# Retention in chunks of 64 on quarters of the matrix array, with query products ahead of the head transposes

## The chip, the cores and the metric

The kernel runs on one core of a Trainium2 chip. A core has a matrix engine (TensorE, PE in the profile) with an array of 128 x 128 cells, a vector engine (VectorE, DVE), a scalar engine (ScalarE, ACT), GpSimd (POOL), and a queue engine for transfers (SyncE, SP). Working memory (SBUF) has 128 partitions; TensorE writes its results to banks of PSUM, from which VectorE and ScalarE read. The metric is the device time of one execution in microseconds.

## What is computed

The reference is a trunk of two layers over 1024 frames of 1024 channels. Layer 0 holds a state-space branch and a retention branch, layer 1 a convolution module. The change touches retention alone:

```python
CHUNK = 64; RET_HEADS = 8; RET_DK = 64; RET_DV = 128
scores = einsum('bnihd,bnjhd->bnhij', qc, kc) * intra       # within a chunk of 64
intra_out = einsum('bnhij,bnjhe->bnihe', scores, vc)
kv = einsum('bnjhd,jh,bnjhe->bnhde', kc, k_dec, vc)         # one state per chunk
# state_step: s -> chunk_decay * s + kv_n, and chunk n sees the state before it
cross = einsum('bnihd,ih,bnhde->bnihe', qc, q_dec, s_prev)
out = intra_out + cross                                      # then normalised per head
```

Queries and keys are rotated by position first, and the normalised output is multiplied by a SiLU gate. All of it is f32.

## The kernel before, in words

The eight heads are worked on in four pairs. A pair's keys lie in a tile of 128 partitions (two heads of 64 channels) by 1024 frames, and so do its queries. The value tiles `vt` have frames on partitions.

`retention` (line 936) runs over the pairs. For each it takes the finished rotated keys and queries of `ret_proj`, emits six pieces of `weight_low`, starts `ret_proj` of the next pair up to its key products, and then emits `ret_heads`. `weight_low` (line 224) is work for layer 1: it loads half a weight block, casts it on ScalarE, subtracts on GpSimd and stores the low part, in two buffers for each tile. The next pair's query products come only when the loop comes round.

`ret_proj` (line 974) makes 48 products of 512 columns for the keys and 48 for the queries (`mm_k`, `mm_q`, lines 276 to 278: each block is multiplied as high and low parts, three products a block). VectorE scales them (line 987), four transfers swap halves of the rotation (line 996), GpSimd multiplies by the tables and VectorE adds (line 1003).

`ret_heads` (line 1079) works on blocks of 128 frames, that is two chunks:

- eight transposes of the keys (`ktp`, line 1088), each group of four multiplied by the key decay on VectorE (line 1090);
- the products `kv` (line 1107): a block's 128 frames are contracted, the output has 64 rows a head, so the two heads take the two column halves of the array;
- the recurrence of the states `S` on VectorE (lines 1115 and 1117), seven links, one per block;
- the scores `sp` (line 1124): 64 channels are contracted, so the two heads take the two row halves; VectorE masks them into `sc` (line 1130). The mask is zero where a frame of the first chunk would see the second;
- the outputs `ro`: state products on row halves (line 1154), then value products on the whole array (line 1159), each half of the sequence in two PSUM banks, one a head;
- per head and half: mean and variance (lines 1168 and 1169), the root on ScalarE (line 552), normalising (line 1174), transposes back (`rt`, line 1182), the multiplication by the gates `grl` (line 1185), and a store (line 1188).

Every engine works through its instructions in order. The order is fixed when the kernel is built: a planner takes instructions by their place in the program, the earlier first, and fills an engine's idle time, as it estimates it, with later ones that are ready. `issue_after(x)` puts an instruction behind x where both are on the same engine; `chained` fixes the order of a list of products. Five PSUM banks (`ps_aux`) serve all the tiles of `ret_heads`, three (`ps_mm`) the projections. After retention come the gated linear unit of the state-space branch (`mm_glu`), the output projection and layer 1.

Of the kernel before, what the change touches and what calls it, by code (L numbers as in the profile page):

```python
# [19 lines left out]
P = 128  # L20
D = 1024
T = 1024
# [35 lines left out]
class Trunk:  # L58
# [877 lines left out]
    def retention(self, st):  # L936
# [7 lines left out]
        self.mask = r0.tile([P, NH, P], F32, name="retmask")  # L944
        nc.sync.dma_start(self.mask[:], A["ret_mask"])
        self.g128 = r0.tile([P, 4], F32, name="g128")
        nc.sync.dma_start(self.g128[:], A["ret_g128"])
        self.kdec = r0.tile([P, NH, 64], F32, name="kdec")
# [3 lines left out]
        ahead = None  # L952
        for pair in range(4):
            cur = list(ahead or self.ret_proj(pair))[-1]
            if pair == 0:
                with ExitStack() as vst:
                    V = self.ret_values(self.pool("vp", 1, stack=vst))
                self.rp = self.pool("ret", 1, stack=st)
                ry = self.pool("retl", 1, stack=early, side="right")
            with ExitStack() as held:  # L960
# [12 lines left out]

# [46 lines left out]
    def ret_values(self, vp):  # L1020
# [56 lines left out]
        return lambda p, b, hh: vt[p // 2][b // 4][:, b % 4, (2 * (p % 2) + hh) * P:(2 * (p % 2) + hh + 1) * P]  # L1077

    def ret_heads(self, pair, K, Q, qadds, V, turned):
# [4 lines left out]
        for hf in range(2):  # L1084
            ps = self.bank(f"ktp{hf}_{pair}")
            for b in range(4):
                t0 = (4 * hf + b) * P
                nc.tensor.transpose(ps[:, b * P:(b + 1) * P], K[:, t0:t0 + P], self.ident[:])
            kd = self.kdec[:, 2 * pair:2 * pair + 2, :].rearrange("p h d -> p (h d)")
            self.last_kt = v.tensor_tensor(kt[:, 4 * hf:4 * hf + 4, :], ps[:].rearrange("p (b d) -> p b d", b=4),  # L1090
                                           kd.unsqueeze(1).broadcast_to([P, 4, P]), op=ALU.mult)
# [6 lines left out]
        S = rp.tile([P, 8, P], F32, name=f"S_{pair}", tag="S", bufs=1)  # L1098
        for hf in range(2):
            ps = self.bank(f"kv{hf}_{pair}")  # L1100
            for b4 in range(4):
                b = 4 * hf + b4
                if b == 7:
                    continue
                for hh in range(2):
                    r = slice(64 * hh, 64 * hh + 64)
                    nc.tensor.matmul(ps[r, b4 * P:(b4 + 1) * P], kt[:, b, r], V(pair, b, hh),
                                     start=True, stop=True)
            for b4 in range(4):
                b = 4 * hf + b4  # L1110
                if b == 7:
                    continue
                kv = ps[:, b4 * P:(b4 + 1) * P]
                if b == 0:
                    v.tensor_copy(S[:, 1, :], kv)
                else:
                    v.scalar_tensor_tensor(S[:, b + 1, :], S[:, b, :], self.g128[:, pair:pair + 1], kv,
                                           op0=ALU.mult, op1=ALU.add)

        self.masked = [None, None]  # L1120
        sc = [rp.tile([P, 8, P], F32, name=f"sc{hh}_{pair}", tag=f"sc{hh}", bufs=1) for hh in range(2)]
        for hf in range(2):
            sps = [self.bank(f"sp{hf}{hh}_{pair}") for hh in range(2)]
            self.chained(nc.tensor.matmul(sps[hh][:, b4 * P:(b4 + 1) * P],
                                          K[64 * hh:64 * hh + 64, (4 * hf + b4) * P:(4 * hf + b4 + 1) * P],
                                          Q[64 * hh:64 * hh + 64, (4 * hf + b4) * P:(4 * hf + b4 + 1) * P],
                                          start=True, stop=True)
                         for b4 in range(4) for hh in range(2))
            for hh in range(2):
                self.masked[hf] = v.tensor_tensor(  # L1130
                    sc[hh][:, 4 * hf:4 * hf + 4, :], sps[hh][:].rearrange("p (b i) -> p b i", b=4),
                    self.mask[:, 2 * pair + hh, :].unsqueeze(1).broadcast_to([P, 4, P]), op=ALU.mult)

# [4 lines left out]
        for hh in range(2):  # L1138
            h = 2 * pair + hh
            gt = rp.tile([P, T], F32, name=f"grl_{h}", tag="grl", bufs=3)  # L1140
# [4 lines left out]
        for hf in range(2):  # L1145
            pss = [self.bank(f"ro{hf}_{2 * pair + hh}") for hh in range(2)]

            def products():
                for b4 in range(4):
                    b = 4 * hf + b4  # L1150
                    for hh in range(2):
                        r = slice(64 * hh, 64 * hh + 64)
                        if b:
                            yield nc.tensor.matmul(pss[hh][:, b4 * P:(b4 + 1) * P], Q[r, b * P:(b + 1) * P],
                                                   S[r, b, :], start=b4 == (hf == 0), stop=False)
                for hh in range(2):
# [615 lines left out]
```

## Time and profile before

| | us |
|---|---|
| median of three runs (1176.0 to 1176.86) | 1176.35 |
| the profiled execution, first to last instruction | 1173.9 |
| TensorE busy in it | 1161.3 |
| VectorE busy | 910.5 |
| GpSimd busy | 713.5 |
| ScalarE busy | 545.1 |

Only the span of the profiled execution is given; the runs' time lies 2.45 us above it. In the rows of the profile a line number (L1159) points into the kernel, `ro<-v,sc` names the tile written and the tiles read, `64*128` the part of the array used (rows times columns), and a bracket the idle time of the engine before the instruction, with what ended it. PEld is TensorE's loading of the stationary operand, which runs beside its products. In a table of stretches each row is a window in us, the busy time of the engines with their instructions, the clock that TensorE was granted (1.00 is full), the share of the transfer engines, and GB/s. One transfer engine's queue is written SPq.

### The profile page before, as it was taken

Reading aid. Unit: us, or ns where it says so; the run is one execution under the profiler, and the core shown is the slowest. Engines: PE = TensorE matmul, PEld = TensorE weight load, DVE = VectorE, ACT = ScalarE, POOL = GpSimd, SP = SyncE. Lnnn points to the kernel's source line nnn. Section 1 sums busy time; section 2 is a strip of 40 time slices with the busy share of each in tenths; the row PEclk is TensorE's granted clock in tenths of the full one; section 3 lists DMA queues with packets and bytes.
Section 4 is the critical chain, followed back from the end, with each engine's and each line's share of the span. In section 5 each row is a group of like instructions: output and inputs, shape, how many; then the busy total and the mean of one; then the engine's idle time right before and its main releaser. Section 6 shows DMA issues by size and latency. Waiting matters only on the chain.

```text
span 1173.9 us, 17492 instructions
## 1 busy us (share of the span) xinstructions
PE 1161.3 (99%) x6150; PEld 965.5 (82%) x6150; DVE 910.5 (78%) x1507; ACT 545.1 (46%) x821; POOL 713.5 (61%) x507
## 2 busy tenths in 40 slices
PE   9999999999999999999999999999999999999997
PEld 7888888888888888887788888888888888888887
DVE  7875789999717475689777888479999999999643
ACT  7212343332226642123645544367756678544662
POOL 2049999888843245664444034348894689977742
PEclk9999999999999999999999999999999999999999
DMA  9353378778789765765988468965448553357863
GB/s 344 109 178 109 134 270 312 272 269 282 273 307 325 268 228 192 251 190 180 362 313 304 160 220 268 309 232 188 161 158 306 216 182 132 134 176 243 281 247 138
DMA packets 131192, 270.66 MB, mean 231 GB/s; under 512 B 12832, under 2 KB 41760, under 8 KB 130976
## 3 DMA queue, kind: packets, MB, share of 16 engines
q1 hardware_dynamic: 129952, 265.35, 66.5%
q10 hardware_dynamic: 1152, 4.19, 0.9%
q8 instruction: 48, 0.79, 0.3%
q14 instruction: 40, 0.33, 0.1%
HBM read 193.54 MB, written 71.76 MB: 226 GB/s over the span
## 4 chain that ended last, share of the span: by engine, by line
PE 91%; DMA 4%; DVE 2%; SPq 1%; ACT 1%; POOL 1%; issue 1%; DVEq 0%; POOLq 0%; ACTq 0%
PE mm_g L277 8%; PE mm_g L278 8%; PE mm_g L276 7%; PE mm_w L278 4%; PE mm_w L277 4%; PE mm_w L276 4%; PE mm_a L278 2%; PE mm_b L277 2%; PE mm_a L276 2%; PE mm_b L278 2%; PE mm_a L277 2%; PE mm_b L276 2%; PE mm_u L278 2%; PE mm_oc L278 2%; PE mm_u L277 2%; PE mm_oc L277 2%
## 5 line engine op out<-in xcount | busy, mean ns | idle before, releaser
L1461 DVE SCALAR_TENSOR_TENSOR cv<-u,convw,cv 128x512 f32<-128x512 f32 x358 | 244.7, 750 | 5.0 <-ACT cv L1447 3.5
L1441 POOL TENSOR_TENSOR tp<-tp,tp 128x512 f32<-128x512 f32 x104 | 138.9, 1338 | 28.7 <-ACT tp L1440 23.4
L278 PE MATMUL mm_g<-xh,wl_g 128*128 128x512 f32 x256 | 100.8, 394 | 0.0
L277 PE MATMUL mm_g<-xl,wh_g 128*128 128x512 f32 x256 | 100.7, 394 | 0.0
L276 PE MATMUL mm_g<-xh,wh_g 128*128 128x512 f32 x256 | 100.5, 393 | 0.0
L1440 ACT ACTIVATE tp<-u,convw 128x512 f32<-128x512 f32 x104 | 69.6, 713 | 9.6 <-POOL tp L1441 9.4
L277 PEld LDWEIGHTS mm_g<-xl,wh_g 128*128 128x128 f32 x256 | 48.1, 188 | 11.2 <-issue 1.6
L278 PEld LDWEIGHTS mm_g<-xh,wl_g 128*128 128x128 f32 x256 | 48.0, 188 | 10.5
L276 PEld LDWEIGHTS mm_g<-xh,wh_g 128*128 128x128 f32 x256 | 48.1, 188 | 9.6
L278 PE MATMUL mm_oc<-zh,wl_woc 128*128 128x512 f32 (+1 forms) x152 | 54.5, 360 | 0.2 <-DMA wl_woc<-lo_woc 0.2
L276 PE MATMUL mm_oc<-zh,wh_woc 128*128 128x512 f32 (+1 forms) x152 | 54.3, 362 | 0.0
L277 PE MATMUL mm_oc<-zl,wh_woc 128*128 128x512 f32 (+1 forms) x152 | 54.0, 357 | 0.0
L276 PE MATMUL mm_glu<-yh,wh_glu 128*128 128x512 f32 x128 | 50.0, 392 | 1.3 <-ACT sg L1250 1.3
L277 PE MATMUL mm_u<-xl,wh_u 128*128 128x512 f32 x128 | 50.1, 391 | 1.0 <-DVE xl L390 0.9
L276 PE MATMUL mm_g<-h1h,wh_cg 128*128 128x512 f32 x128 | 50.3, 393 | 0.0
L276 PE MATMUL mm_a<-h1h,wh_ca 128*128 128x512 f32 x128 | 50.3, 393 | 0.0
L278 PE MATMUL mm_b<-h1h,wl_cb 128*128 128x512 f32 x128 | 50.3, 393 | 0.0
L232 ACT CAST lh<-lf 128x512 fp32r<-128x512 f32 x32 | 19.5, 618 | 65.9 <-DMA lf<-w_c 59.3
L278 PE MATMUL mm_a<-h1h,wl_ca 128*128 128x512 f32 x128 | 50.0, 391 | 0.0
L277 PE MATMUL mm_glu<-yl,wh_glu 128*128 128x512 f32 x128 | 50.0, 392 | 0.0
L278 PE MATMUL mm_g<-h1h,wl_cg 128*128 128x512 f32 x128 | 49.9, 390 | 0.0
L277 PE MATMUL mm_g<-h1l,wh_cg 128*128 128x512 f32 x128 | 49.9, 390 | 0.0
(811 smaller groups left out, 3637.3 us busy)
## 6 DMA issues: line engine op xcount, KB each, us to landing
wf_g<-w_ab SPq DMA_DIRECT2D x16, 512.0 KB, 5.4
a<-w_out SPq DMA_DIRECT2D x32, 256.0 KB, 4.4
ws<-a SPq DMA_DIRECT2D x32, 256.0 KB, 4.8
lf<-w_c SPq DMA_DIRECT2D x32, 256.0 KB, 5.3
wf_p<-ws SPq DMA_DIRECT2D x16, 512.0 KB, 4.1
wf_cb<-w_c SPq DMA_DIRECT2D x16, 512.0 KB, 4.9
wf_ca<-w_c SPq DMA_DIRECT2D x16, 512.0 KB, 4.7
wl_cb<-lo_cb SPq DMA_DIRECT2D x16, 512.0 KB, 3.4
```

What stands on the lines that cost most here:

```text
L232: self.nc.scalar.copy(hi[:], f[:])
L276: nc.tensor.matmul(ps, wh[:, kb, :], xh, start=start, stop=False)
L277: nc.tensor.matmul(ps, wh[:, kb, :], xl, start=False, stop=False)
L278: self.last_mm = nc.tensor.matmul(ps, wl[:, kb, :], xh, start=False, stop=stop)
L1440: nc.scalar.mul(sk[:], u[:, k:k + HALF], cw[:, nb, k:k + 1])
L1441: gp.tensor_tensor(s0[:], s0[:], sk[:], op=ALU.add)
L1461: v.scalar_tensor_tensor(dst[:], *tap, accs_[i][:], op0=ALU.mult, op1=ALU.add)
```

## The change

Retention goes from blocks of 128 frames to chunks of 64, as in the reference:

- The scores of chunk c are made by 64 x 64 pieces of keys and queries; head 0 takes the upper left quarter of the array and head 1 the lower right. Both heads' scores lie in one tile `sc`, head 0 on the lower partitions and head 1 on the upper, and in one bank for eight chunks. The mask is a table of 64 columns a pair, without zeros.
- `kv`, the state products and the value products are 64 x 64 in the stationary operand and 128 columns in the moving one, so each takes a quarter; four successive ones take four different quarters. `kv` uses four banks a pair.
- `S` has 15 states, and the recurrence 15 links with the decay of 64 frames.
- A value product needs a chunk's values on the partitions of its head's scores. For odd chunks of head 0 and even chunks of head 1 they lie on the other half, so `crossed` copies them into a tile `vx` (one buffer) with four transfers a pair, after the values for pair 0 and after `ret_heads` of the pair before for the others.
- Statistics of both halves are emitted before the first three normalisations; then the next pair's query products with all that follows them (`fill`); then two transposes groups, the fourth normalisation, and the last two groups.
- The six low parts a pair go into two groups of three, one where all six stood and one behind the key transposes (`last_kt`), with three buffers.
- The gates have two buffers instead of three, the statistics' small tiles four instead of two; the tables for mask and key decay shrink.

```diff
-            held.enter_context(self.tc.issue_after((self.last_rs if pair else self.last_sum).ins))
-            for k in range(LOWS * pair // 3, LOWS * (pair + 1) // 3) if pair < 3 else ():
-                self.weight_low(ry, k, (("la", "lb"), ("la", "lb")), 2, nc.gpsimd)
+            def lows(n, behind):
+                with self.tc.issue_after(behind.ins):
+                    for k in range(n * LOWS // 6, (n + 1) * LOWS // 6) if pair < 3 else ():
+                        self.weight_low(ry, k, (("la", "lb"), ("la", "lb")), 3, nc.gpsimd)
             def turned():
+                lows(2 * pair + 1, self.last_kt)
...
+            lows(2 * pair, self.last_rs if pair else self.last_sum)
...
-            self.ret_heads(pair, *cur, V, turned)
+            cur = self.ret_heads(pair, *cur, V, turned, lambda: list(ahead)[-1] if ahead else None)
+            if pair < 3:
+                self.crossed(pair + 1)
...
+    def crossed(self, pair):
+        d, i = pair // 2, pair % 2
+        self.vx = self.r0.tile([P, 8, P], F32, name=f"vx{pair}", tag="vx", bufs=1)
+        for h in range(2):
+            for hh in range(2):
+                to, of = slice(64 * hh, 64 * hh + 64), slice(64 - 64 * hh, 128 - 64 * hh)
+                self.nc.sync.dma_start(self.vx[to, 4 * h:4 * h + 4, :],
+                                       self.vt[d][h][of, :, (2 * i + hh) * P:(2 * i + hh + 1) * P])
...
+            kvs = [self.bank(f"kv{hf}{par}_{pair}") for par in range(2)]
+            self.chained(nc.tensor.matmul(kvs[c % 2][half(hh), col(c)], kt[half(c % 2), c // 2, half(hh)],
+                                          V(pair, c, hh)[half(c % 2)], start=True, stop=True)
+                         for c in cs for hh in range(2))
...
+            sps = self.bank(f"sp{hf}_{pair}")[:].rearrange("p (c i) -> p c i", c=8)
+            self.chained(nc.tensor.matmul(sps[half(hh), c % 8, :], K[half(hh), tok(c)], Q[half(hh), tok(c)],
                                           start=True, stop=True)
+                         for c in range(8 * hf, 8 * hf + 8) for hh in range(2))
...
+                            yield nc.tensor.matmul(out(c, hh), Q[half(hh), tok(c)], S[half(hh), c - 1, :],
+                                                   start=c in (2, 1, 8, 9), stop=False)
+                for c in cs:
+                    for hh in range(2):
+                        yield nc.tensor.matmul(out(c, hh), sc[half(hh), c, :], V(pair, c, hh, True)[half(hh)],
+                                               start=False, stop=c % 8 > 5)
...
+        on00, on01, on10 = (normed(*a) for a in todo[:3])
+        nxt = fill()
+        last_ro = turn(0, 1, on01, last_ro)
+        last_ro = turn(0, 0, on00, last_ro)
+        on11 = normed(*todo[3])
+        last_ro = turn(1, 0, on10, last_ro)
+        turn(1, 1, on11, last_ro)
```

More of the change, by code (lines that the diff above doesn't have):

```diff
@@ L951, in retention @@
         nc.sync.dma_start(self.reps[:], A["ret_eps"])
-        ahead = None
+        cur = list(self.ret_proj(0))[-1]
         for pair in range(4):
-            cur = list(ahead or self.ret_proj(pair))[-1]
             if pair == 0:
@@ L1076, in ret_values, with value, ret_heads @@
                     self.y_pass(vp, cb)
-        return lambda p, b, hh: vt[p // 2][b // 4][:, b % 4, (2 * (p % 2) + hh) * P:(2 * (p % 2) + hh + 1) * P]
-    def ret_heads(self, pair, K, Q, qadds, V, turned):
+        def value(p, c, hh, own=False):
+            d, h, b, i = p // 2, c // 8, c // 2 % 4, p % 2
+            if own and c % 2 != hh:
+                return self.vx[:, c // 2, :]
+            return vt[d][h][:, b, (2 * i + hh) * P:(2 * i + hh + 1) * P]
+        return value
+    def crossed(self, pair):
[6 more added lines that the diff above has]
+                                       self.vt[d][h][of, :, (2 * i + hh) * P:(2 * i + hh + 1) * P])
+    def ret_heads(self, pair, K, Q, qadds, V, turned, fill):
         nc, rp = self.nc, self.rp
@@ L1096, in ret_heads @@
         turned()
-        S = rp.tile([P, 8, P], F32, name=f"S_{pair}", tag="S", bufs=1)
+        S = rp.tile([P, 15, P], F32, name=f"S_{pair}", tag="S", bufs=1)
+        half = lambda i: slice(64 * i, 64 * i + 64)
         for hf in range(2):
[L1100 to L1115, printed above, removed]
+            kvs = [self.bank(f"kv{hf}{par}_{pair}") for par in range(2)]
+            cs = [c for c in range(8 * hf, 8 * hf + 8) if c < 15]
+            col = lambda c: slice(c // 2 % 4 * P, (c // 2 % 4 + 1) * P)
+            self.chained(nc.tensor.matmul(kvs[c % 2][half(hh), col(c)], kt[half(c % 2), c // 2, half(hh)],
+                                          V(pair, c, hh)[half(c % 2)], start=True, stop=True)
+                         for c in cs for hh in range(2))
+            for c in cs:
+                kv = kvs[c % 2][:, col(c)]
+                if c == 0:
+                    v.tensor_copy(S[:, 0, :], kv)
@@ L1116, in ret_heads @@
                 else:
-                    v.scalar_tensor_tensor(S[:, b + 1, :], S[:, b, :], self.g128[:, pair:pair + 1], kv,
+                    v.scalar_tensor_tensor(S[:, c, :], S[:, c - 1, :], self.g64[:, pair:pair + 1], kv,
                                            op0=ALU.mult, op1=ALU.add)
         self.masked = [None, None]
-        sc = [rp.tile([P, 8, P], F32, name=f"sc{hh}_{pair}", tag=f"sc{hh}", bufs=1) for hh in range(2)]
+        sc = rp.tile([P, 16, 64], F32, name=f"sc_{pair}", tag="sc", bufs=1)
@@ L1122, in ret_heads @@
         for hf in range(2):
[L1123 to L1126, printed above, removed]
+            sps = self.bank(f"sp{hf}_{pair}")[:].rearrange("p (c i) -> p c i", c=8)
+            tok = lambda c: slice(c * 64, (c + 1) * 64)
@@ L1139, in ret_heads @@
             h = 2 * pair + hh
[L1140 removed]
+            gt = rp.tile([P, T], F32, name=f"grl_{h}", tag="grl", bufs=2)
             with self.tc.issue_after(self.masked[0].ins):
@@ L1148, in products @@
             def products():
-                for b4 in range(4):
-                    b = 4 * hf + b4
+                cs = range(8 * hf, 8 * hf + 8)
+                out = lambda c, hh: pss[hh][half(c % 2), c // 2 % 4 * P:(c // 2 % 4 + 1) * P]
+                for c in cs:
                     for hh in range(2):
[L1152 to L1156, printed above, removed]
-                    for b4 in range(4):
-                        b = 4 * hf + b4
-                        yield nc.tensor.matmul(pss[hh][:, b4 * P:(b4 + 1) * P], sc[hh][:, b, :],
-                                               V(pair, b, hh), start=False, stop=b4 == 3)
+                        if c:
+                            yield nc.tensor.matmul(out(c, hh), Q[half(hh), tok(c)], S[half(hh), c - 1, :],
+                                                   start=c in (2, 1, 8, 9), stop=False)
+                for c in cs:
+                    for hh in range(2):
+                        yield nc.tensor.matmul(out(c, hh), sc[half(hh), c, :], V(pair, c, hh, True)[half(hh)],
+                                               start=False, stop=c % 8 > 5)
             last_ro = self.chained(products())
```

70 lines of the change are left out of this document (35 added, 35 removed).

## The prediction

> **What bounds the kernel now.** I read the page first, then the busy time by stretches, then TensorE's instructions in order of time.
>
> ```profile
> span 1173.9 us, 17492 instructions
> PE 1161.3 (99%) x6150; PEld 965.5 (82%) x6150; DVE 910.5 (78%) x1507; ACT 545.1 (46%) x821; POOL 713.5 (61%) x507
> ...
> PE 91%; DMA 4%; DVE 2%; SPq 1%; ACT 1%; POOL 1%; issue 1%; DVEq 0%; POOLq 0%; ACTq 0%
> ```
>
> TensorE is busy for 99% of the span, and 91% of the chain that ended last is its work. In the stretches of 25 us it runs 112 products of 512 columns back to back, or 0.223 us each; only retention (448 to 592 us) leaves something over:
>
> ```profile
> 475.00:500.00 25.00, 25.00 (x192) 21.23 (x191) 16.20 (x45) 3.37 (x6) 17.57 (x13) 1.00 0.81 253
> 525.00:550.00 25.00, 23.96 (x154) 20.15 (x153) 24.03 (x70) 7.59 (x16) 11.29 (x8) 1.00 0.63 184
> 550.00:575.00 25.00, 24.05 (x190) 20.13 (x188) 20.46 (x60) 9.21 (x13) 9.55 (x7) 1.00 0.85 312
> 600.00:625.00 25.00, 25.00 (x112) 20.73 (x111) 16.74 (x25) 11.54 (x18) 12.59 (x6) 1.00 0.92 323
> ```
>
> The waits there, from TensorE's order of time, sum to 3.0 us, and VectorE ends two of the three:
>
> ```profile
> 544.83 1.06 PE L1182 MATMUL rt<-ident,on 128*128 128x128 f32 x8 [1.04 <-DVE on L1174]
> 553.95 1.75 PE L1107 MATMUL kv<-v,kt 128*64 128x128 f32 x28 [0.67 <-DVE kt L1090]
> 576.05 0.50 PE L276 MATMUL mm_glu<-yh,wh_glu 128*128 128x512 f32 x1 [1.33 <-ACT sg L1250]
> ```
>
> So the end moves by what TensorE is spared, less any wait that appears. TensorE is just as full after retention, so what is won there should reach the end undiminished.
>
> **What the small products cost now.** Pair 0 in order of time, with one line that stands for the filler from the next pair's projection:
>
> ```profile
> 447.49 1.75 PE L1107 MATMUL kv<-v,kt 128*64 128x128 f32 x28
> 449.17 1.38 PE L1124 MATMUL sp<-qrot,krot 64*128 64x128 f32 x18
> 450.48 0.51 PE L276 MATMUL mm_q<-xh,wh_q 128*128 128x512 f32 x1
> ...
> 452.77 1.04 PE L1124 MATMUL sp<-qrot,krot 64*128 64x128 f32 x13
> ...
> 454.53 2.05 PE L1159 MATMUL ro<-v,sc 128*128 128x128 f32 x16
> 456.51 1.16 PE L1154 MATMUL ro<-S,qrot 64*128 64x128 f32 x16
> 457.60 2.05 PE L1159 MATMUL ro<-v,sc 128*128 128x128 f32 x16
> 459.41 0.48 PE L276 MATMUL mm_q<-xh,wh_q 128*128 128x512 f32 x1
> ```
>
> Every f32 product stands as two instructions (line 1107 makes 14 a pair, the row shows 28). I take times from start to start. Sixteen full-array instructions last 454.53 to 456.51, 1.98 us; sixteen on halves of the array, two at a time, last 1.09 us. If a step of the array (one set of parallel instructions) lasts t and a change of the array's partition s, then 16t + s = 1.98 and 8t + s = 1.09: t = 0.111, s = 0.20 us. The block kv agrees roughly: 14t + s = 1.75 against 1.68.
>
> A pair takes 447.49 to 450.48 and 452.77 to 459.41, or 9.63 us. In steps that is kv 14, scores 16, state products 14, values 32: 76t = 8.44 us, with about seven changes of partition.
>
> **Four at a time?** No row of before has 64x64 quarters. The nearest are four column strips of S5:
>
> ```profile
> 108.80 0.45 PE L882 MATMUL kp<-Mr,s_s_cbr 128*32 128x128 f32 x8
> 109.04 0.42 PE L883 MATMUL kp<-Mi,s_s_cbi 128*32 128x128 f32 x8
> 109.39 0.50 PE L277 MATMUL mm_g<-xl,wh_g 128*128 128x512 f32 x1
> 108.79 0.18 PEld L882 LDWEIGHTS kp<-Mr,s_s_cbr 128*32 128x32 f32 x8 [0.17 <-issue]
> ```
>
> Eight start within 0.24 us, and all sixteen with the change of partition behind them last 0.59 us (4t + s = 0.64). Four run at once, 0.03 us each, so issue is no floor. Row pairs (sp, ro) and column pairs (kv) run together too. I therefore take 0.111 us for four quarters; the other bound is two at a time.
>
> *A rule that speaks against it.* The Trainium skill (TensorE: Matmul & The Clock Gate, Part 3: Packing small matmuls, The mechanism) says that a weight load overlaps running products only where the row group differs; two quarters of one row group would then be taken in turn, which is the last rival below. Here the trace differs: the eight loads of kp share all rows and were under way within 0.18 us.
>
> **The change, part by part.**
>
> *Products.* kv has 15 chunks x 2 heads = 30 products, 60 instructions, 15 steps. State products: 30, 15 steps. Values: 32 products of half the contraction and half the tokens, 16 steps instead of 32. Scores: 32 products with 64 columns, but only on the two diagonal quarters: 32 short steps. How long is a short step?
>
> ```profile
> L1159 PEld LDWEIGHTS ro<-v,sc x128: 185/192/193, 454.5 to 570.2; 128*128 128x128 f32 x128
> L1107 PEld LDWEIGHTS kv<-v,kt x112: 132/137/138, 447.5 to 555.3; 128*64 128x64 f32 x112
> ...
> 34.95 1.73 PE ss L547 x16
> ```
>
> The last line, from the chain, is a product with 64 moving columns and 128 columns of weights: 0.108 us each, so halving the moving side alone wins nothing. But the load of 64 columns is 0.055 us shorter than that of 128 (137 against 192 ns), half a step, and here both sides are halved. Bounds 0.055 and 0.111 us; I take 0.055, that is 16t. Sum after: 15 + 15 + 16 + 16 = 62t = 6.88 us. All four kinds now have one partition; with one filler in between there are four changes, 0.80 us. 7.68 against 9.63: 1.95 us a pair, **8 us** in four pairs (bounds: 12.6 us lost if quarters run two at a time, 0.9 us won if score steps stay long; both are rivals below).
>
> *VectorE.* The recurrence grows from 7 links to 15, the masks halve from four instructions to two:
>
> ```profile
> L1117 DVE SCALAR_TENSOR_TENSOR S<-S,g,kv x24: 336/347/348, 449.0 to 565.4; 128x128 f32<-128x128 f32 x24
> L1130 DVE TENSOR_TENSOR sc<-sp,retmask x16: 680/684/692, 450.8 to 566.3; 128x512 f32<-128x512 f32 x16
> ```
>
> 8 x 0.347 - 2 x 0.684 = +1.4 us a pair. From the first kv half (8t = 0.9 us) the chain ends after 0.9 + 15 x 0.347 + two masks 1.4 = 7.5 us; TensorE has kv, scores and the first half of the outputs in that time (15t + 16t + 15t = 5.1 us), so it needs about 2.4 us of projection between them, as much as the 2.29 us it puts there now (450.48 to 452.77). In pairs 0 and 1 that cover is there, and VectorE is a third idle (16.20 of 25). In 525 to 550 us it has 24.03 of 25: there I let one pair's 1.4 us come through as a wait, **+1.5 us**. The key decay and the normalisations keep their counts, and the smaller tables are loaded once, long before use.
>
> *Queries in front of the transposes.* All 48 query products of the next pair are the same work. Of them some 38 (8.5 us) are left when the outputs are done, where now 6.66 us pass before the first transposes:
>
> ```profile
> 466.07 1.06 PE L1182 MATMUL rt<-ident,on 128*128 128x128 f32 x8 [0.27 <-DVE mv L1169]
> L1168 DVE BATCH_NORM_STATS2 st<-ro 128x6 f32<-128x128 f32 x64 | 14.3, 279 | 1.4 <-PE ro L1159 1.4
> L1174 DVE TENSOR_SCALAR on<-ro,mv,rs 128x128 f32<-128x128 f32 x64 | 21.7, 403 | 0.3
> ```
>
> Three normalisations must now precede the first transpose (3/4 x 21.7/4 = 4.1 us, behind 3.6 us of statistics): 7.7 us, which 8.5 us cover. Without that cover it costs the difference to the gate products that stand in, up to 1.3 us as for sg above. What is late next is the product with the gates and its store. Cost: nothing. The three waits of before may go (-3.0) or stay; I keep them.
>
> *Copies and low parts.*
>
> ```profile
> L996 SPq DMA_DIRECT2D kswp<-kraw x16: 507/583/616, 354.1 to 522.2; - x16
> kswp<-kraw SPq DMA_DIRECT2D x16, 128.0 KB, 3.9
> ...
> DMA to landing us min/median/max: 2.3/3.3/7.7
> L232 ACT CAST lh<-lf 128x512 fp32r<-128x512 f32 x32 | 19.5, 618 | 65.9 <-DMA lf<-w_c 59.3
> ```
>
> Each pair adds four copies within SBUF of 128 KB, as large as those of kswp: 4 x 0.58 = 2.3 us of SP's queue, landing 3 to 8 us later. They wait for the previous pair's last value product (the tile has one buffer); behind them in SP's queue stand the swapped copies of the next keys and the low parts' loads. They are read a whole pair's projection later (96 x 0.223 = 21 us), which hides them; without it TensorE would wait up to 7.7 us. The low parts are the same 18 loads, casts (0.618 us) and subtractions, spread wider and with a third buffer; nothing on TensorE reads them here, their loads only fill DMA time. The gates' loads with two buffers wait for both stores, 20 us ahead of use. All taken as nothing.
>
> **Sum.** In the profiled execution's terms 1173.9 - 8.0 + 1.5 = 1167.4 us. The median of the runs, 1176.35, lies 2.45 above that span, so the forecast is **1169.9 us**, 6.5 less.
>
> **The rivals.**
>
> 1. *The short score step does not halve.* Then scores cost 32t, 1.8 us more a pair: 1169.9 + 7.1 = 1177.0. The product of line 547 speaks for it, the shorter weight load against it. The Trainium skill (TensorEngine Tiling (Array Packing), Gotcha 1: PSUM Pressure) gives a mechanism with the same price: different row tiles cannot use one PSUM bank at once, and the two heads' scores now share a bank. No row tells: each row pair of before writes two banks.
>
> 2. *The recurrence is uncovered (the other side).* Place: between kv and the second half of the state products, in every pair. The eight links more are 8 x 0.347 = 2.8 us; where the order fixed beforehand holds no projection for them TensorE waits that long. Price 4 x 2.8 = 11.2: 1176.35 - 8 + 11.2 = 1179.5. It decides from 2.0 us a pair on, where it eats the gain. For it speaks pair 3, where the seven links took 8.4 us because other VectorE work stood between; against it, that projections are free to be put there.
>
> ```profile
> 557.41 0.29 DVE L1115 COPY S<-kv 128x128 f32<-128x128 f32 x1
> ...
> 565.03 0.73 DVE L1117 SCALAR_TENSOR_TENSOR S<-S,g,kv 128x128 f32<-128x128 f32 x2
> ```
>
> 3. *Quarters run two at a time.* 30 + 30 + 32 + 16 = 108t = 12.0 + 0.8 against 9.63, +3.2 us a pair: 1176.35 + 12.6 = 1189. Break-even lies at 79 steps. The rows of kp speak against it.
>
> 4. *The waits of before go as well.* 1176.35 - 8.0 - 3.0 = 1165.3; for it speak the earlier queries, against it VectorE's 24.03 of 25.
>
> **How the numbers follow.** Forecast 0.52 (its own range 1166 to 1174), rivals in order 0.14, 0.14, 0.10, 0.10. The measurement tells 0.2%, 2.35 us. Faster: forecast and rival 4, 0.62. Same: rival 1 and the part of rival 2 with half of the chain covered, 0.14 + 0.04 = 0.18. Slower: rest of rival 2 and rival 3, 0.20. The range 1164 to 1180 leaves out rival 3 and the thin ends.
>
> **What would show it.** kv, ro and sp rows of form 64*64, 60 to 64 a pair; kv and ro blocks of 0.03 us an instruction (0.055 is rival 3); score blocks of 0.9 us for 32 instructions (1.8 is rival 1); 60 recurrence links, and no TensorE wait on S of over 1 us (rival 2 would show about 2.8 us each); VectorE's sum up by some 5.6 us. Wrong it would be above all if TensorE's idle time in retention grows by more than the 8 us.

## The result, and the profile after

The changed kernel takes 1192.22 us (median of four runs, 1188.89 to 1192.88), the kernel before 1176.61 us beside it. The ratio is 1.0118, with an interval of 1.0097 to 1.0138: slower by 1.2%, or about 14 us, where 6.5 us less was forecast. The medians lie 15.6 us apart, the two profiled executions 17.2 us. The page's head, the busy sums and the chain's shares:

```profile
span 1191.1 us, 18558 instructions
...
PE 1161.4 (98%) x6662; PEld 965.3 (81%) x6662; DVE 927.1 (78%) x1531; ACT 539.4 (45%) x817; POOL 711.4 (60%) x507
...
PE 81%; DMA 9%; DVE 4%; SPq 2%; POOL 2%; issue 2%; ACT 1%; DVEq 0%; ACTq 0%; POOLq 0%
```

TensorE's share of the chain fell from 91% to 81%, and transfers and VectorE took its place. Where, the stretches show (busy time of the engines in their fixed order, then the granted clock):

```profile
475.00:500.00 25.00, 25.00 (x331) 21.16 (x330) 19.35 (x54) 1.61 (x3) 9.30 (x6) 1.00 0.73 207
500.00:525.00 25.00, 23.06 (x186) 19.11 (x185) 18.34 (x43) 7.88 (x14) 23.51 (x16) 0.93 0.68 207
525.00:550.00 25.00, 20.25 (x218) 16.74 (x218) 23.41 (x71) 7.81 (x15) 9.30 (x6) 0.89 0.72 205
550.00:575.00 25.00, 19.84 (x242) 16.89 (x244) 17.96 (x40) 3.28 (x5) 5.99 (x5) 0.84 0.69 240
575.00:600.00 25.00, 18.32 (x141) 15.17 (x134) 19.05 (x65) 10.87 (x17) 8.55 (x5) 0.86 0.86 300
600.00:625.00 25.00, 25.00 (x112) 20.69 (x111) 23.03 (x22) 10.76 (x17) 14.22 (x8) 1.00 0.93 336
```

From 500 to 600 us TensorE stands still for 100 - 81.47 = 18.5 us, against 3.0 before. The clock, 1.00 in all of these rows before, is 0.84 to 0.93. Little is lost elsewhere.

The array's part did what was forecast. Pair 0 in TensorE's order of time (start and duration first, then engine, line and operation):

```profile
448.13 1.85 PE L1125 MATMUL kv<-v,kt 64*64 64x128 f32 x58
...
449.93 1.09 PE L1141 MATMUL sp<-qrot,krot 64*64 64x64 f32 x30
450.95 0.50 PE L276 MATMUL mm_q<-xh,wh_q 128*128 128x512 f32 x1
...
453.67 0.97 PE L1141 MATMUL sp<-qrot,krot 64*64 64x64 f32 x26
...
457.93 0.38 PE L1170 MATMUL ro<-v,sc 64*64 64x128 f32 x2
458.24 0.50 PE L278 MATMUL mm_q<-xh,wl_q 128*128 128x512 f32 x1
```

2.82 and 4.57 us make 7.39 us for the pair (7.68 forecast, 9.63 before). What was lost is in the rows with a bracket:

```profile
509.28 0.63 PE L1195 MATMUL rt<-ident,on 128*128 128x128 f32 x4 [1.94 <-DVE rs L553]
...
545.76 1.94 PE L1195 MATMUL rt<-ident,on 128*128 128x128 f32 x8 [4.32 <-DVE mv L1180]
550.06 0.63 PE L277 MATMUL mm_glu<-yl,wh_glu 128*128 128x512 f32 x1
550.49 0.63 PE L278 MATMUL mm_glu<-yh,wl_glu 128*128 128x512 f32 x1
...
571.67 2.13 PE L1166 MATMUL ro<-S,qrot 64*64 64x128 f32 x27 [5.17 <-DVE S L1133]
584.26 1.97 PE L1195 MATMUL rt<-ident,on 128*128 128x128 f32 x8 [6.56 <-DVE on L1189]
```

Two things cost here: the waits, and what follows them. The eight transposes after the 4.32 us take 1.94 us where such a group took 1.06 us before, and the products of 512 columns behind them start 0.43 us apart instead of 0.223: half speed. The books for TensorE from its first `kv` to its first `mm_w` (start 447.5 and 643.3 before, 448.1 and 659.2 after): 15.3 us longer = 15.1 of waits (the brackets sum to 18.4 against 3.3) - 6.7 of small products (31.8 against 38.5, from start to start) + 6.9 in the rows of the transposes and the projections, which are the same work as before at a lower clock.

**Why pair 3 waits.** VectorE names `S` and the normalisations, but is itself held up. Its queue in pair 3, then SP's:

```profile
566.32 0.69 DVE L1273 SCALAR_TENSOR_TENSOR sg<-sg,yg 128x512 f32<-128x512 f32 x1 [2.93 <-POOL yg L1268]
566.93 1.11 DVE L1133 SCALAR_TENSOR_TENSOR S<-S,g,kv 128x128 f32<-128x128 f32 x3
569.35 0.69 DVE L1216 TENSOR_TENSOR yl<-yf,yh 128x512 fp32r<-128x512 f32 x1 [1.31 <-ACT yh L1214]
...
576.69 0.69 DVE L233 TENSOR_TENSOR lh<-lf,lh 128x512 fp32r<-128x512 f32 x1 [1.54 <-ACT lh L232]
```

```profile
553.55 0.32 SPq L1209 DMA_DIRECT2D yr_d<-grl  x1
558.20 0.33 SPq L1154 DMA_DIRECT2D grl<-gr_d  x1
558.62 0.38 SPq L1209 DMA_DIRECT2D yr_d<-grl  x1
...
563.68 0.32 SPq L1154 DMA_DIRECT2D grl<-gr_d  x1
564.10 0.85 SPq L1245 DMA_DIRECT2D yf<-yn_d  x2
```

Read the second block first. With two gate buffers pair 3's first load of gates (558.20) needs pair 2's first store to have landed, 4.6 us after its issue. Pair 2's second store was ready at 556.3 but stands behind that load and goes at 558.62; the second load then needs that store, until 563.68. So two store latencies come one after the other, and the next stage's rows `yf` behind them go at 564.10 (558.25 before). ScalarE's cast of the rows waits for them, GpSimd's `yg` waits for `yn` from the same queue, and the work on VectorE that needs both (`sg`, `yl`) stands between the links of `S`. Pair 2's wait has another cause and is followed below.

**Why pair 1 waits.** The same happens two pairs earlier, with pair 0's stores:

```profile
486.92 0.38 SPq L1209 DMA_DIRECT2D yr_d<-grl  x1
487.40 0.51 SPq L1001 DMA_DIRECT2D kswp<-kraw  x1
494.05 0.32 SPq L1154 DMA_DIRECT2D grl<-gr_d  x1
494.42 1.79 SPq L1001 DMA_DIRECT2D kswp<-kraw  x3
```

Pair 1's second load of gates needs pair 0's second store and goes 7.1 us behind it; three of the four swapped copies of the next keys stand behind that load. GpSimd takes the copies up at 500.55, VectorE waits 2.13 us for the product and starts to add it at 504.39, and the normalisation behind it is late for the transposes at 509.28 (the wait of 1.94 us).

### The profile page after: what moved, and what is told of

It reads as the page before. It is cut to its first block, busy times and chain, and to the rows that moved or that the text cites. A ratio compares the mean times of both kernels' runs of the same rounds, so it can differ in the third digit from the quotient of the medians.

```text
span 1191.1 us, 18558 instructions
## 1 busy us (share of the span) xinstructions
PE 1161.4 (98%) x6662; PEld 965.3 (81%) x6662; DVE 927.1 (78%) x1531; ACT 539.4 (45%) x817; POOL 711.4 (60%) x507
## 4 chain that ended last, share of the span: by engine, by line
PE 81%; DMA 9%; DVE 4%; SPq 2%; POOL 2%; issue 2%; ACT 1%; DVEq 0%; ACTq 0%; POOLq 0%
PE mm_g L277 7%; PE mm_g L278 7%; PE mm_g L276 7%; PE mm_w L278 4%; PE mm_w L277 4%; PE mm_w L276 4%; DMA lf<-w_c 3%; PE mm_a L278 2%; PE mm_b L278 2%; PE mm_b L277 2%; PE mm_a L277 2%; PE mm_a L276 2%; PE mm_b L276 2%; PE mm_u L278 2%; PE mm_oc L278 2%; PE mm_u L277 2%
## 5 line engine op out<-in xcount | busy, mean ns | idle before, releaser
L1268 POOL TENSOR_TENSOR yg<-yg,yn 128x512 f32<-128x512 f32 x16 | 23.2, 1455 | 56.6 <-DMA yn<-yn_d 17.6
L278 PE MATMUL mm_glu<-yh,wl_glu 128*128 128x512 f32 x128 | 51.4, 401 | 0.0
L276 PE MATMUL mm_u<-xh,wh_u 128*128 128x512 f32 x128 | 49.2, 396 | 1.3 <-ACT xh L389 1.3
```

Of the source, the lines that this page charges most:

```text
L276: nc.tensor.matmul(ps, wh[:, kb, :], xh, start=start, stop=False)
L278: self.last_mm = nc.tensor.matmul(ps, wl[:, kb, :], xh, start=False, stop=stop)
L1268: gp.tensor_tensor(yg[:], yg[:], yn[:], op=ALU.mult)
```

## The experiments

All ratios are to the kernel before, run beside each. Three kernels leave work out, so that their output is not the reference's: e_nocopy (the copies), e_short and e_short_links (8 of the 16 value products a pair).

| kernel | ratio, interval | us |
|---|---|---|
| e_rest: the change without the quarters | 1.0003, 0.999 to 1.0015 | 1178.67 |
| e_before_fill: before + queries in front | 0.9989, 0.9978 to 1.0001 | 1176.40 |
| e_before_gates2: before + two gate buffers | 0.9992, 0.9982 to 1.0002 | 1176.16 |
| e_quarters: quarters and copies alone | 1.0111, 1.0093 to 1.0128 | 1190.45 |
| e_low6: quarters + queries in front | 1.0082, 1.0067 to 1.0097 | 1186.78 |
| e_gates3_early: that + low parts in threes, third buffer | 1.0012, 1.0000 to 1.0024 | 1179.59 |
| e_early: that + two gate buffers | 1.0003, 0.9993 to 1.0012 | 1178.03 |
| changed kernel: that + late normalisations | 1.0118, 1.0097 to 1.0138 | 1192.22 |
| e_gates3: changed, three gate buffers | 1.0078, 1.0058 to 1.0099 | 1187.39 |
| e_hold: changed, pair 3's transposes later | 1.0151, 1.0125 to 1.0178 | 1195.60 |
| e_nocopy: changed, without the copies | 1.0111, 1.0092 to 1.0131 | 1190.86 |
| e_after_y1: changed + one row buffer | 1.0034, 1.0021 to 1.0047 | 1181.60 |
| e_y1: e_early + one row buffer | 1.0026, 1.0014 to 1.0037 | 1180.89 |
| e_pool: e_early, low parts on GpSimd | 1.0055, 1.0035 to 1.0075 | 1183.59 |
| e_before_pool: before, the same | 0.9985, 0.9976 to 0.9995 | 1176.03 |
| e_short: before, shorter array part | 0.9976, 0.9966 to 0.9985 | 1174.48 |
| e_links: before, longer VectorE chain | 0.9996, 0.9983 to 1.0009 | 1177.33 |
| e_short_links: both | 0.9987, 0.9976 to 0.9998 | 1175.63 |

### The changed kernel's two parts: gates and normalisations

**e_gates3** gives the third gate buffer back:

```diff
-            gt = rp.tile([P, T], F32, name=f"grl_{h}", tag="grl", bufs=2)
+            gt = rp.tile([P, T], F32, name=f"grl_{h}", tag="grl", bufs=3)
```

> The changed kernel with three buffers for the gates again, nothing else. Theory 1 (queue): with two buffers the gate loads of the last pair stand in SP's queue until the stores of the pair before are done, and the loads behind them come late; that makes the 5.2 us wait of the outputs for the recurrence in the last pair. Then that wait goes, with some 2 us of lowered clock behind it: about 1185 us. Theory 2 (order): the normalisations put off make the waits before the transposes, and the planner still puts a single gate product there: 1192 us as the changed kernel. Theory 3 (recurrence): the 15 links on VectorE are late by themselves: 1192 us.

**e_early** puts each normalisation right behind its statistics and turns half 0 and half 1 in the order of before; the next queries stay in front:

```diff
-                ons.append((h, hf, ps, mv, rs))
+                on = rp.tile([P, 4, P], F32, name=f"on_{h}_{hf}", tag="on", bufs=3)
+                for b4 in range(4):
+                    v.tensor_scalar(on[:, b4, :], ...)
+                ons.append(on)
...
+        for hf in range(2):
+            for hh in (1, 0):
+                last_ro = turn(hf, hh, todo[2 * hf + hh], last_ro)
```

> The changed kernel with each normalisation right behind its statistics, as in the kernel before; two gate buffers, queries in front, low parts in threes as in the changed kernel. Theory 2 (order): the planner now puts 37 gate products instead of 1 between the last pair's outputs and its transposes, so the waits of 4.3 and 6.6 us go with the lowered clock behind them: about 1177 us. Theory 1 (queue): the wait for the recurrence stays, the rest only moves: 1188 to 1192 us. Theory 3 (recurrence): 1188 us or more.

**e_gates3_early** has both.

> Both: three gate buffers and normalisations behind their statistics. If theories 1 and 2 both hold, all large waits go and the eight microseconds of saved array time show: about 1169 us. If theory 3 holds, the waits for the recurrence in the last two pairs stay: 1180 us or more.

The buffer is worth 0.40% (4.7 us; the two intervals just overlap), the early normalisations 1.15% (13.5 us), and both together no more than the second alone. The 1169 us expected of both did not come: pair 2's wait stays (4.27 us in that kernel), and 2.09 us for `S`.

In e_gates3 the four swapped copies of pair 1 go at 486.90, and the wait of 1.94 us is gone; pair 2's transposes start at 540.88 against 545.76 in the changed kernel. So a good part of what the buffer is worth lies in pair 1, where nothing was expected. In pair 3 the wait for `S` did not go, but fell from 5.17 us to 2.59 and 1.56. The stores are still parted (547.59 and 551.25), but only one of pair 3's two loads of gates waits for either of them.

SP's queue in e_early says why one cures what the other cures:

```profile
552.88 0.93 SPq L1203 DMA_DIRECT2D yr_d<-grl  x2
...
555.54 0.32 SPq L1154 DMA_DIRECT2D grl<-gr_d  x1
...
557.40 0.38 SPq L1154 DMA_DIRECT2D grl<-gr_d  x1
557.88 1.16 SPq L1239 DMA_DIRECT2D yf<-yn_d  x2
```

The two stores go together, although there are two buffers as in the changed kernel, and the rows go at 557.88, as before. In the changed kernel pair 2's last two groups of transposes are four each, 3.4 us apart (551.56 and 555.00) with 13 products between them, since the fourth normalisation comes late; in e_early they are one block of eight. So it is the late fourth normalisation that parts the stores here, and the missing buffer that makes the parting dear. e_early's waits of over 1 us on TensorE:

```profile
543.67 1.94 PE L1192 MATMUL rt<-ident,on 128*128 128x128 f32 x8 [4.27 <-DVE mv L1180]
...
565.22 1.36 PE L1166 MATMUL ro<-S,qrot 64*64 64x128 f32 x27 [1.68 <-DVE S L1133]
...
568.90 0.43 PE L1166 MATMUL ro<-S,qrot 64*64 64x128 f32 x2 [1.33 <-DVE sc L1144]
```

Pair 3's 5.17 and 6.56 us have become 3.0, and pair 1's wait is gone. Pair 2's wait is as in the changed kernel, though theory 2 let it go too. In e_early the small products take 31.9 us against 38.5 before, but TensorE waits 9.0 us against 3.3, and the time is no better than before.

**e_rest** is the kernel before with everything but the quarters and copies (late normalisations and two gate buffers too).

> The kernel before with all of the change but the quarters: chunks stay 128 long and there are no crossed copies, but the next queries' products stand in front of the transposes, the normalisations behind both turns' statistics, the low parts in two groups of three a pair and the gates' rows in two buffers. Theory: what loses the time is the quarters' own queue, that is VectorE's 15 links a pair in place of 7, and an array that comes to the waits earlier; without them the late normalisations have cover, and the time is 1176 to 1180 us. Rival: the new order of the work loses the time by itself, whatever the array does; then it is 1184 to 1192 us here as well.

The time is the theory's, 1178.67: without the quarters the new order costs nothing. (The theory's reason, the 15 links, is tested under e_links.) Two of the four groups of pair 2 stand alone here too, but with 4 products between them, the stores go together (554.00), and the rows go at 559.44. What is cheap on its own is dear with the quarters. Why the planner puts 13 products there with the quarters and 4 without was not found out.

**e_before_gates2** and **e_before_fill** make one of these edits each in the kernel before: the gates' `bufs=3` becomes `bufs=2`; `nxt = fill()` is put in front of the first transposes.

> The kernel before, with two buffers for the gates' rows instead of three, and nothing else. Theory: in the changed kernel the two buffers cost 4.8 us, by the loads in SP's queue that wait for stores to end and hold up the rows of the next stage behind them. If that alone is enough, this kernel loses 2 to 6 us against the one before. Rival: it costs only where VectorE is late already, that is with the two turns' normalisations behind both turns' statistics; then this kernel is within 1 us of the one before.

> The kernel before with the next queries in front of the transposes alone. Its first transposes waited 0.3 us only, so there is nothing to win: 1176 to 1178 us. Were it much faster, the queries would be a gain of their own, and were it slower, a cost that I had put at nothing.

Neither moves the time. For the gates the expectation's second reading held.

**e_hold** leaves the changed kernel whole but emits pair 3's first two groups of transposes later:

```diff
-        last_ro = turn(0, 1, on01, last_ro)
-        last_ro = turn(0, 0, on00, last_ro)
+        with self.at(self.tc.cur_priority + (220 if pair in (3,) else 0)):
+            last_ro = turn(0, 1, on01, last_ro)
+            last_ro = turn(0, 0, on00, last_ro)
```

> The changed kernel, with one thing different: in pair 3 the first two groups of transposes are emitted at a later place, so the planner puts 24 products of the next stage in front of them instead of 1. Theory 1: the wait of 6.56 us at these transposes comes from the order the planner wrote, in which TensorE has nothing between the outputs and the transposes. Then it falls to under 2 us, the clock stays at 0.93 or above from 575 us on, and the time is 1180 to 1186 us; the wait of 5.17 us for S stays. Theory 2: the order doesn't matter, since all that could stand there waits for the same late rows; then another wait of 4 us or more takes its place, and it is 1189 to 1193 us.

The wait at the transposes is gone, and another one stands behind them, as in the second theory, but the time lies above its range. The stores are still parted (550.62 and 555.50). TensorE and ScalarE:

```profile
588.24 0.80 PE L276 MATMUL mm_glu<-yh,wh_glu 128*128 128x512 f32 x1 [8.56 <-ACT sg L1273]
```

```profile
583.91 0.62 ACT L232 CAST lh<-lf 128x512 fp32r<-128x512 f32 x1 [7.74 <-DMA lf<-w_c]
```

So 24 products in front of the transposes gain nothing while the loads are late. That the parted stores make this weight load late too was not followed.

**e_nocopy** has no `crossed` copies.

> The changed kernel without the crossed copies: the value products that read them read the other half of the value tile instead, so the output is not the reference's. TensorE's order is the same. Theory: the copies cost nothing, as predicted, 1190 to 1193 us. Rival: the 16 transfers in SP's queue, 4 MB with their reads and writes, make the rows and gates behind them late; then it is 1182 to 1188 us.

0.07% less than the changed kernel, far inside the two intervals. The copies are not the cause.

### What the quarters do by themselves

**e_quarters** is the changed kernel with three gate buffers, early normalisations, the queries behind the transposes and six low parts in two buffers, that is, close to the quarters and the copies alone; **e_low6** adds the queries in front.

```diff
-            lows(2 * pair, self.last_rs if pair else self.last_sum)
+            for n in (2 * pair, 2 * pair + 1):
+                lows(n, self.last_rs if pair else self.last_sum)
...
-        nxt = fill()
...
-        return nxt
+        return fill()
```

> Chunks of 64 on quarters alone: three gate buffers, normalisations behind their statistics, the next queries after the transposes, six low parts at one place in two buffers, all as in the kernel before. The planner puts 2 query products between the first pair's outputs and its transposes where the kernel before had 27, so a wait of some 5 us should stand there (with lowered clock, 6 to 7 us): about 1175 us if the rest is as in the run with both repairs; 1185 us or more if the recurrence itself is what is late (theory 3).

> As e_gates3_early (quarters, three gate buffers, normalisations behind statistics, queries in front), but six low parts at one place in two buffers as before. It differs from e_quarters by the queries in front alone, and from e_gates3_early by the low parts alone. If the queries in front are what e_quarters lacked: about 1180 us as e_gates3_early, so that the low parts count for nothing; if the low parts are: 1190 us as e_quarters.

The quarters alone lose 1.1%. That is in the range that theory 3 gave, but waits on `S` are only 2.3 of TensorE's 17.4 us of waits in retention. The largest part is one place, in pair 0:

```profile
458.20 0.39 PE L276 MATMUL mm_q<-xh,wh_q 128*128 128x512 f32 x1
466.43 1.94 PE L1192 MATMUL rt<-ident,on 128*128 128x128 f32 x8 [7.84 <-DVE on L1185]
```

The planned order of TensorE there, and in the changed kernel:

```
e_quarters       ro 62, mm_q 2,  rt 8, mm_q 27, rt 8, mm_q 8, mm_k 48
changed kernel   ro 62, mm_q 37, rt 12, mm_k 31, rt 4, mm_k 17
```

Two products cover nothing; with the queries in front there are 37, and this wait is gone. That is what the edit is for, and it can't be seen in the kernel before, where 27 products stood there anyway. The gain from e_quarters to e_low6 is 0.3%, with intervals that overlap. From e_low6 to e_gates3_early, 0.7%, the low parts go into groups of three and get a third buffer; which of the two counts was not tested. Both kernels have a wait of 4.27 us in pair 2; ahead of it TensorE waits 5.7 us in eight places in e_low6 and 1.0 us in two in e_gates3_early. The loads behind this were not followed.

### Pair 2's wait

In e_early VectorE's low parts `yl` stand in front of pair 2's statistics and wait 2.5 us for rows that were issued at 523.2 and cast from 531.0 on. But the rows are not all of it: in e_gates3 VectorE's rows show no wait from pair 2's first state (518.40) to these transposes, and TensorE waits 4.34 us all the same. **e_pool** gives every second of these subtractions to GpSimd (`gp if not halves and kb % 2 else v`); **e_before_pool** is the same edit in the kernel before.

> The kernel of the run e_early with every second low part of the gated unit's input (yl) subtracted on GpSimd, not on VectorE. In pair 2 the transposes still wait 4.3 us for VectorE, whose queue holds four yl pieces in between the statistics. Theory 4 (VectorE's queue in pair 2): that wait falls below 1 us and the clock behind it stays full, so about 6 us less than e_early: 1172 us. If the wait comes from the loads of that input (transfers), not from VectorE, it stays: 1178 us.

> The kernel before with the same yl pieces on GpSimd, as a control: its own wait there was 1.0 us. Theory 4: 1 to 2 us less than before at most, 1175 to 1177 us. If GpSimd is simply a better place for them, it gains as much as the other run.

e_pool is slower than e_early by 0.5%, which neither theory gave. The subtractions now stand behind GpSimd's rotation work, which is later still:

```profile
536.28 0.80 PE L277 MATMUL mm_glu<-yl,wh_glu 128*128 128x512 f32 x1 [3.47 <-POOL yl L1210]
...
543.38 1.94 PE L1192 MATMUL rt<-ident,on 128*128 128x128 f32 x8 [3.32 <-DVE on L1185]
```

**e_y1** and **e_after_y1** give one tile of these rows its own buffer:

```diff
-                            f2 = self.wp.tile([P, 2, HALF], F32, ..., tag="wf", bufs=3)
+                            f2 = (lp.tile([P, 2, HALF], F32, ..., tag="wfy", bufs=1) if h == 0 and kb in (4,) else
+                                  self.wp.tile([P, 2, HALF], F32, ..., tag="wf", bufs=3))
```

> The kernel of e_early, and one tile of the next stage's input rows (the rows of blocks 4 and 5, first half) has a buffer of its own, so its load need not wait until a buffer that the weights use is free. The planner now puts 10 products of the next stage in front of pair 2's first transposes instead of 23. Theory 1: in e_early pair 2's transposes come at 543.7 us because VectorE's low parts of these rows stand in its queue ahead of the statistics and wait for a load that was issued at 523.2 and landed at 531.0. Then that load lands before 524 here, pair 2's waits on VectorE (4.27 and 0.72 us) fall to under 2 together, and the time is 1172 to 1176 us. Theory 2: VectorE itself has too much work there, whatever is loaded; then the transposes of pair 2 are ready at 541 or later all the same, TensorE's waits from 525 to 600 us still come to 7 us or more, and the time is 1177 to 1181 us.

> The changed kernel whole (two gate buffers, normalisations behind both turns), with the one extra buffer for the next stage's rows as in e_y1. Theory 1: pair 2's wait of 4.32 us for the transposes goes to under 2, with the lowered clock behind it; pair 3's two waits (5.17 and 6.56 us), which come from the gates' loads and the late normalisations, stay: 1184 to 1189 us. Theory 2 (VectorE's own work): no gain, 1190 to 1194 us.

In e_y1 the rows were not issued earlier (523.72; the swapped copies stand ahead in SP's queue), so the first theory was not tested as meant, but the time followed the second: 1180.89, with waits of 2.59, 0.70, 0.96, 1.65 and 1.39 us from 525 to 600 us. VectorE came to its statistics 5 us earlier, and the wait moved on to ScalarE, whose cast of the late rows stands in front of the roots, and from there back to VectorE:

```profile
532.84 0.62 ACT L1208 CAST yh<-yf 128x512 fp32r<-128x512 f32 x1 [12.13 <-DMA yf<-yn_d]
533.36 0.48 ACT L552 ACTIVATE rs<-mv,reteps 128x4 f32<-128x4 f32 x2
```

```profile
533.69 0.18 DVE L553 RECIPROCAL rs<-rs 128x4 f32<-128x4 f32 x1 [2.49 <-ACT rs L552]
```

e_after_y1 gained 0.84% (9.9 us) on the changed kernel, more than expected, and much of it in pair 3, where nothing was expected: there the two stores go together again (547.79, both) and the rows at 550.83. So two unlike edits, this buffer and the early normalisations, join the same two stores, and with either of them most of the loss goes. e_hold is the control: there too 24 products stand in front of pair 3's transposes, as in e_after_y1, but the stores are parted and nothing is gained.

### A shorter array part and a longer chain, without quarters

**e_short** and **e_links** imitate the quarters' two effects in the kernel before, **e_short_links** has both:

```diff
+                        if b4 in (1, 2):
+                            continue
                         yield nc.tensor.matmul(pss[hh][:, b4 * P:(b4 + 1) * P], sc[hh][:, b, :],
...
+                if b in (1, 2, 4, 5):
+                    v.scalar_tensor_tensor(spare[:], S[:, b, :], self.g128[:, pair:pair + 1], kv,
+                                           op0=ALU.mult, op1=ALU.add)
```

> The kernel before with a shorter array part and nothing else new: of the 16 products of the masked scores with the values a pair, the 8 of each half's second and third block are left out, so the output is not the reference's. That is 8 products of two instructions of about 0.1 us, some 1.6 us a pair and 6.5 us in all, near what the quarters save, with VectorE's work as before. Theory 1: what TensorE gains in this stage is given back, since the waits in pairs 2 and 3 are for loads and VectorE, which don't come earlier; then the waits from 500 to 600 us grow by 4 us or more, and the time is 1174 to 1179 us. Theory 2: the gain stays, and it is the quarters' longer chain on VectorE that costs; then 1170 to 1173 us.

> The kernel before with 4 links more a pair on VectorE, which write a spare tile that nobody reads: 4 by about 0.37 us, 1.5 us a pair, what the changed kernel's VectorE has more a pair (8 links more, two maskings fewer). The array's work is as before. Theory 1: no more than 3 us slower, 1176 to 1180 us, since the array covers it. Theory 2: the longer chain alone does it: 1183 to 1192 us.

> Both of these: the 8 products a pair left out (so the output is not the reference's) and the 4 spare links a pair. It imitates the quarters' two effects on the two engines without the quarters. Theory 1 (shorter array and longer chain meet): it is slower than the sum of the two alone by 3 us or more, 1180 us or above, although the array has 6.5 us less to do. Rival: the effects add up, or neither matters, and it is 1171 to 1178 us; then the quarters' own order on the array (what the planner makes of smaller instructions and the crossed copies) is what costs.

The longer chain costs nothing by itself (-0.2 us). It has 4 links more a pair, which is VectorE's extra work, where the quarters have 8 and two maskings fewer; but in the changed kernel all 15 links stand in pairs 0 to 2 as well, without a wait on `S`. The shorter array part saved 5.2 us (`ro` rows 23.4 us before, 18.2 here) and the kernel gained 3.0, at the edge of theory 1's range: TensorE's waits grew from 3.3 to 5.9 us, in pairs 2 and 3 again. From TensorE's order of e_short:

```profile
549.86 1.10 PE L1184 MATMUL rt<-ident,on 128*128 128x128 f32 x8 [1.93 <-DVE on L1176]
...
552.84 1.75 PE L1107 MATMUL kv<-v,kt 128*64 128x128 f32 x28 [1.02 <-DVE kt L1090]
...
564.83 0.93 PE L1154 MATMUL ro<-S,qrot 64*128 64x128 f32 x10 [1.03 <-DVE S L1117]
```

With both it is -1.9 us: the two effects neither meet nor add up to a loss. So neither of the quarters' effects on the two engines explains 14 us. The rival reading is left, that is the order around them: it is shown for pair 0 in e_quarters (by e_low6), for pair 1 (by e_gates3) and for pair 3 (by e_early and e_after_y1, against e_hold). Of 5.2 us that the array was spared, these two kernels gained 3.0 and 1.9.

No kernel that computes the reference beats the kernel before by more: e_early, e_before_fill and e_before_gates2 are the kernel before within 0.2%, and e_before_pool's 0.15% less is too.

## Why the prediction was wrong

*Four quarters at a time; the short score step.* Right. The scores' 30 instructions of 449.93 to 450.95 less 0.20 us for the change of partition make 15 steps of 0.055 us. Pair 0 spared 2.24 us against 1.95 forecast. Over all pairs the small products' own time fell by 6.7 us in the changed kernel and by 8.2 in e_y1, whose waits disturb them less (8 forecast). Rival 1 and rival 3 (which the prediction also calls "the last rival") are out; that 1189 lay near the measured time was chance.

*"What is won there should reach the end undiminished."* Wrong, and here the reasoning failed first. TensorE was 99% busy because the waits of pairs 2 and 3 were just covered. Pair 2 shows it: from its first state to its first transposes VectorE takes 21.6 us before (523.22 to 544.83), 23.0 in the changed kernel (522.81 to 545.76), 24.3 in e_early and 22.5 in e_gates3. What the array is spared in between went into TensorE's wait there, which grew from 1.04 us to 4.3 in all three. e_short kept 3.0 of 5.2 us.

*"+1.5 us" for a wait that comes through.* This is the term that failed: the waits grew by 15.1 us, and the work behind them ran 6.9 us longer. It was sized by VectorE's extra work, and e_links shows that this work costs nothing by itself. What counted was what stands in front of `S` and the statistics in its queue and waits for others. Rival 2 had the place half right (one wait for `S`, 5.17 us, in pair 3 alone), but its mechanism was the number of links, of which there were as many in pairs 0 to 2 without any wait over 1 us on `S`.

*"Gates' loads with two buffers wait for both stores, 20 us ahead of use. All taken as nothing."* Right for use, wrong for the queue: nobody waited for the gates, but the loads stood in SP's queue in front of the rows in pair 3 and of the swapped copies in pair 1. The prediction had even named what stands behind the copies in that queue and did not ask it here. Alone the two buffers cost nothing (e_before_gates2), with the quarters and late normalisations 4.7 us.

*Queries in front of the transposes: nothing.* The queries cost nothing and are worth some 0.3% with the quarters. But the cover of 8.5 us was worked out for pair 0 and taken for all. Pairs 1 and 2 have 15 query products behind their outputs, and pair 3 has no next pair: there the planner put one product in front of the transposes. The late normalisations that came with this edit cost 13.5 us, by far the most; with three gate buffers they cost 7.8, and without the quarters nothing (e_rest).

*Copies: nothing.* Right (e_nocopy). *Low parts: nothing.* Wrong the other way: three and three with a third buffer are worth 0.7% once the quarters are there. *VectorE's sum up by 5.6 us.* It rose by 16.6; the sum also rises when an instruction takes longer, and e_links, with 5.6 us more to do, had 909.0 against 910.5, so it decides nothing.

*Not in the prediction at all:* the clock. It had read 1.00 in every row before and did not ask what a new wait does to it. Some 6.9 of the 15.3 us are that.

What stays open: why the quarters make the planner part pair 2's transposes by 13 products, which load holds e_low6 up, and how pair 2's wait divides between VectorE's own work and the late rows.

## What to carry to other kernels

An engine that is busy for 99% of the time does not have to be the only bound: before a saving is booked in full, look for the waits that are just covered, and ask what sets the time at which they end. When an edit takes away a buffer, follow the transfer that now waits and list what stands behind it in its queue, above all where a store and the next load alternate. A cover that is worked out for the first round of a loop must be worked out for the last one too, where the next round's work is missing.

## What was not expected of the hardware

Waits of a few microseconds can lower the granted clock (0.84 to 0.93 in the stretches from 500 to 600 us), and products after them run at half speed for 3 to 6 us. After the 4.32 us at 545.76 the products of 512 columns are 0.43 us apart until 551.3. After only 1.94 us at 509.28 the transposes still ran at full speed, and then the products from 510.5 to 513.4 were 0.43 us apart; yet e_short's wait of 1.93 us was followed by full speed throughout. The Trainium skill (TensorE: Matmul & The Clock Gate, Part 1: The HAM clock gate, What's actually happening) tells of a free-running window of about 3.4 us and of half clock after one idle window. The half speed and the chance of where the wait falls agree with that; that a wait of 1.94 us could be enough does not, if an idle window is one without any work.

Four 64x64 quarters run at once: the 58 `kv` instructions from 448.13 to 449.73 go at 0.028 us each. The Trainium skill (the same page, Part 3: Packing small matmuls, The mechanism) has weight loads overlap only where the row group differs; here two of every four share their rows, and by that rule we would expect about half the pace. The measurement decides. Nor did it matter that two heads' scores go to one PSUM bank from different row halves: 0.055 us a step.
